# First layer's second MLP product as seven half-size products, and two hand-overs in the MLPs written in another order

## The chip, the cores and the metric

The kernel runs as one program on one core of a Trainium2 chip. The metric is the device time of one execution in microseconds (us). Engines work side by side: TensorE (PE, with the weight loads PEld), VectorE (DVE), ScalarE (ACT), GpSimd (POOL) and SyncE (SP), and 16 DMA engines that all queues share. DMAs are started from SP's, ACT's and POOL's instruction streams. Each engine works through its own instructions in order; a wait at the head of such a stream holds up everything behind it.

## The reference

A two-layer decoder trunk over 1024 tokens with 1024 features. Each layer is a token mixer, an MLP and a gated embedding, each with a norm ahead and a sum behind. Cut to what matters here (per layer `i`):

```python
D_MODEL, SEQ, DEPTH = 1024, 1024, 2
D_FF = 4 * D_MODEL
for i in range(DEPTH):
    hn = rms_norm(h, norm_mix[i])
    y = attention_mixer(hn, ...) if i % 2 == 0 else recurrent_conv_mixer(hn, ...)
    h = h + y
    hn = rms_norm(h, norm_mlp[i])
    h = h + jnp.square(jax.nn.relu(hn @ w_mlp_in[i])) @ w_mlp_out[i]
    hn = rms_norm(h, norm_ple[i])
    h = h + (p[i] @ w_ple_proj[i]) * jax.nn.sigmoid(hn @ w_ple_gate[i])
return rms_norm(h, norm_final)
```

All operands are float32. "The first MLP matrix" is `w_mlp_in` (1024 by 4096), "the second" `w_mlp_out` (4096 by 1024).

## The kernel before

**Tiles.** Everything is held feature-major: 8 blocks of 128 features by 1024 tokens (`h[m]`), and 32 such blocks for the hidden layer. To keep float32 accuracy on TensorE each operand is split into a rounded high part (ScalarE, `hi`, L76) and the rest (VectorE, `lo`, L79, or L89 for weights), and one product of a 128x128 weight block and 512 tokens is three matmuls of 128x512: high by high, high by low, low by high (`mm3`, L92 to L97). A bank is one 128x512 accumulator of PSUM; there are 8 in turn.

**The plain MLP, first layer** (`mlp`, L348). `up` multiplies the input by `w_m1` block by block (48 matmuls a block), scales by the norm (L364), squares what is positive (L365) and splits into `hh`, `hl`. After five blocks eight rounds follow, each with 8 row blocks by two halves of the tokens by four hidden blocks of the second matrix (192 matmuls, and 16 additions into `h`, L385), and four more blocks of `up` between. In all 1536 matmuls belong to the first matrix and 1536 to the second. Woven in is `s5_prep`, a generator that makes tables for the second layer's recurrent mixer in eight parts ("quads"): small VectorE work, then (`later`, one `next` on) 4 transposes (L1111) and 4 small matmuls (L1115) on TensorE, a copy `kt` out of PSUM, eight small DMAs that place `kt` into a zeroed tile `M` (L1127), and a split of `M` that is written to memory (`spill`, L1045 and L1046).

**The MLP of seven products, second layer.** Both matrix products of the second layer are done as 2x2 block products with seven half-size products in place of eight; the sums that this needs are taken on VectorE. Up: `out_proj_halves` and `up_lead` do what needs the first half of the tokens alone, `up_operands` makes the operands X3, X5, X6 from the second half, `up_first` the first sums of weights (`s12`) and products 5 and 6, `up_rest` the operands X4 and X7, `mlp_up` the 16 pairs of hidden blocks; each pair writes its results z1, z2 and four combinations of them to memory (`o1_d`, `o2_d`, `o4_d`). Down: `mlp_down` reads for each of seven products and eight groups a weight tile `raw` and an operand tile `zr` back, splits both, and does 24 matmuls (4 banks by 2 halves by 3); `more(2)` keeps two operand pairs ahead. That makes 56 steps, 1344 matmuls. Its last four blocks of `h` are finished one after another (L765), each with the split for what follows (`xsplit`, L155) and the sum of squares (L304).

**Order.** TensorE's order is that in which the code is written. The order on the other engines is made at build time by a scheduler that goes by readiness and by the code's order; on the chip it is fixed. Pools of SBUF are stacked on a left and a right side; a tile that takes the place of an older one waits until that is free.

**Behind the MLP** come `ple` (first layer: two weight blocks at once, in four banks, inner loop over the eight input blocks) and `ple_last` (second layer: one block at a time).

Of the kernel before, what the change touches and what calls it, by code (L numbers as in the profile page):

```python
# [8 lines left out]
F32 = mybir.dt.float32  # L9
# [9 lines left out]
P = 128  # L19
# [46 lines left out]
class Trunk:  # L66
# [95 lines left out]
    def run(self):  # L162
        tc, nc, A = self.tc, self.nc, self.A
        pool = tc.tile_pool
        with pool(name="w", bufs=1, side=LEFT) as self.wp, \
# [11 lines left out]
            for l in range(2):  # L177
                if l == 0:
                    self.attention(xp)
                with pool(name=f"md{l}", bufs=6, space=PSUM, reuse_waits="tile") as self.mx, ExitStack() as rs:  # L180
# [4 lines left out]
                    if l == 0:  # L185
                        xq = rs.enter_context(pool(name=f"xq{l}", bufs=1, side=RIGHT, reuse_waits="tile"))
                        hp = hs.enter_context(pool(name=f"h{l}", bufs=1, side=RIGHT, reuse_waits="tile"))
                        sp = self.ss.enter_context(pool(name=f"st{l}", bufs=1, side=RIGHT, reuse_waits="tile"))
                        h, xs, st = self.out_proj(l, xp, hp, xq, sp)
                        nxt.close()  # L190
                        with pool(name=f"hid{l}", bufs=1, side=LEFT, reuse_waits="tile") as dp:
                            xs, st = self.mlp(l, h, xs, st, dp, hp, xq)
                        hs.close()
                    else:
                        with pool(name=f"xa{l}", bufs=1, side=RIGHT, reuse_waits="tile") as xa:
# [16 lines left out]
                        xq = rs.enter_context(pool(name=f"xq{l}", bufs=1, side=RIGHT, reuse_waits="tile"))  # L212
                        with pool(name=f"dn{l}", bufs=1, side=LEFT, reuse_waits="tile") as dn:
                            xs, st = self.mlp_down(l, dn, xq)
# [106 lines left out]
    def out_proj(self, l, xp, hp, xq, sp):  # L321
# [14 lines left out]
        def out(m, n, ps):  # L336
# [9 lines left out]
        return h, xs, st  # L346

    def mlp(self, l, h, xs, st, dp, hp, xq):  # L348
        nc, A = self.nc, self.A
        w1 = A["w_m1"][l * FB : (l + 1) * FB]  # L350
        nb = 5 if l == 0 else 6
        hid, nxs, nst, r = {}, [], self.stats_new((xq, "rstd", 1), (dp, "hl", nb)), []

        def up(fb, n, ps):
            if not r:
                if l:
                    self.log_exp()
                r.append(self.rstd_full(st, xq, dp))
                self.ss.close()
            s = slice(n * H, n * H + H)  # L360
            if fb not in hid:
                hid[fb] = [dp.tile([P, T], F32R, tag=x, bufs=nb, name=x) for x in ("hh", "hl")]
            z = dp.tile([P, H], F32, tag="z", bufs=4, name="z")
            nc.vector.tensor_tensor(z, ps, r[0][:, s], ALU.mult)  # L364
            nc.vector.scalar_tensor_tensor(z, z, 0.0, z, ALU.max, ALU.mult)  # L365
            self.hi(hid[fb][0][:, s], z)
            self.lo(hid[fb][1][:, s], z, hid[fb][0][:, s])

        def up_blocks(f0, f1, lead=1):
            self.blocks([w1[f] for f in range(f0, f1)], xs, f1 - f0, list(range(KB)), lambda m, n, ps: up(f0 + m, n, ps), lead)  # L370

        prep = self.s5_prep() if l == 0 else None
        up_blocks(0, 5, 2)
        for c in range(8):
            if prep:
                next(prep)
            for dp2 in range(4):
                w = self.wtile(A["w_m2"][(l * 8 + c) * 4 + dp2])
                for d in range(2):
                    m = 2 * dp2 + d  # L380
                    col = lambda k: tuple(w[j][:, (k - 4 * c) * 256 + d * P : (k - 4 * c) * 256 + d * P + P] for j in range(2))
                    for n in range(2):
                        s = slice(n * H, n * H + H)
                        ps = self.chains([(w, hid, col, n)], list(range(4 * c, 4 * c + 4)))[0]
                        nc.vector.tensor_tensor(h[m][:, s], ps, h[m][:, s], ALU.add)  # L385
                    if c == 7:
                        nc.sync.dma_start(self.h2_d[m], h[m])
                        nxs.append(self.xsplit(h[m], self.gain(3 * l + 2, m), xq))
                        self.stat_block(nst, h[m])
            for f in range(4 * c, 4 * c + 4):  # L390
                del hid[f]
            if c < 7:
                up_blocks(4 * c + 5, min(4 * c + 9, FB))
        if prep:
            for _ in prep:
                pass
        return nxs, nst
# [8 lines left out]
    def split(self, full, pool, tags, bufs):  # L406

        w = full.shape[-1]
        h, l = [pool.tile([P, w], F32R, tag=t, bufs=bufs, name=t) for t in tags]
        self.hi(h, full)  # L410
        self.lo(l, full, h)
        return h, l
# [90 lines left out]
    def put(self, X, p, k, full, xo):  # L503
        X[p, k] = self.split(full, xo, (f"x{p}{k}h", f"x{p}{k}l"), 1)

    def up_operands(self, l, h, st, xo, X):
# [3 lines left out]
        for p in (7, 4):  # L510
            for k in range(4):
                X[p, k] = [xo.tile([P, H], F32R, tag=f"x{p}{k}{x}", bufs=1, name="x") for x in "hl"]
        for k in range(4):
# [3 lines left out]
            self.put(X, 3, k, b[:, rt], xo)  # L517
            v.tensor_tensor(a[:, rt], a[:, rt], a[:, lt], ALU.subtract)
            self.put(X, 5, k, a[:, rt], xo)
            v.tensor_tensor(b[:, rt], b[:, rt], a[:, rt], ALU.subtract)  # L520
            self.put(X, 6, k, b[:, rt], xo)

    def up_rest(self, h, xo, X):
# [3 lines left out]
        for k in range(4):  # L527
            a, b = h[k], h[k + 4]
            for p, s, x, y in ((4, lt, b[:, lt], b[:, rt]), (7, rt, b[:, rt], a[:, lt])):
                v.tensor_tensor(b[:, s], x, y, ALU.subtract)  # L530
                self.hi(X[p, k][0], b[:, s])
                self.lo(X[p, k][1], b[:, s], X[p, k][0])
# [15 lines left out]
    def up_first(self, l, s0, lead, X):  # L548

        raw, a = self.up_raw(l, 0)  # L550
        s12, ops = self.up_s12(a, s0)
# [6 lines left out]
        return raw, a, s12  # L558

    def mlp_up(self, l, X, up, s0, lead, first):  # L560
# [7 lines left out]
        two = lambda d: d.rearrange("p (b e t) -> p b e t", e=2, t=H)  # L568
        both = lambda t: t.rearrange("p (b t) -> p b t", t=H)

        def pair(mp):
            w, bank, c, z = {}, {p: lead[mp, p] for p in (1, 2, 6, 5) if (mp, p) in lead}, {}, {}
            raw, a, s12 = first if mp == 0 else (*self.up_raw(l, mp), None)
            g, e = mp // 2, mp % 2
# [20 lines left out]
            def out(p):  # L595
# [18 lines left out]
                elif p == 3:  # L614
# [4 lines left out]
                    nc.scalar.dma_start(self.o1_d[g][:, e * H : e * H + H], z1[:, lt])  # L619
                else:  # L620
# [4 lines left out]
                    nc.scalar.dma_start(two(self.o2_d[g])[:, :, e, :], both(z2))  # L625
                    ta, tb = [up.tile([P, 1024], F32, tag="tt", bufs=2, name=f"tt{j}") for j in range(2)]
                    tt(ta[:, lt], z1[:, rt], z1[:, lt], ALU.subtract)
                    tt(ta[:, rt], z2[:, rt], ta[:, lt], ALU.subtract)
                    tt(tb[:, lt], z2[:, rt], z1[:, rt], ALU.subtract)
                    tt(tb[:, rt], z2[:, lt], ta[:, rt], ALU.subtract)  # L630
                    for j, t in enumerate((ta, tb)):
                        nc.gpsimd.dma_start(two(self.o4_d[g])[:, 2 * j : 2 * j + 2, e, :], both(t))

            for p in (1, 6, 2, 5, 7, 3, 4):
                if (mp, p) not in lead:
# [3 lines left out]
                    for k in range(4):  # L639
                        self.mm3(bank[b], [o[:, k * P : k * P + P] for o in w[p]], X[p, k], k == 0 and p == b, k == 3, p != b)  # L640
                out(p)

        for mp in range(FB // 2):
            pair(mp)

    def mlp_down(self, l, dn, xq):
# [3 lines left out]
        lt, rt = slice(0, H), slice(H, T)  # L650
        z_d = {1: (self.o1_d, 0), 2: (self.o2_d, 0), 3: (self.o2_d, 1), 5: (self.o4_d, 0), 6: (self.o4_d, 1), 7: (self.o4_d, 2), 4: (self.o4_d, 3)}
# [25 lines left out]
        def operands():  # L677

            for p in (1, 2):
                for g in range(8):  # L680
# [19 lines left out]
        gen, ahead = operands(), []  # L700
# [14 lines left out]
        h, nxs, nst = [], [], self.stats_new((xq, "rstd", 1), (dn, "zr", 3))  # L715
# [7 lines left out]
        for p in (1, 2):  # L723
            for g in range(8):
                step(b1, p == 1 and g == 0, g == 7, p == 2)
                if p == 1 and g in (3, 4):
                    for m in range(g * 4 - 12, g * 4 - 8):
                        h.append(dn.tile([P, T], F32, tag=f"h{m}", bufs=1, name="h"))
# [32 lines left out]
        more(2)  # L761
        for j in range(4):
# [1329 lines left out]
```

## Time and profile before

| | us |
|---|---|
| median of 3 runs (2612.85 to 2615.89) | 2614.22 |
| the profiled execution | 2615.06 |
| its span, first to last instruction | 2613.2 |
| TensorE busy | 2527.2 (97%) |
| VectorE busy | 1693.9 (65%) |
| ScalarE busy | 978.9 (37%) |
| mean granted TensorE clock | 0.988 of full speed |

Stages on the span's clock, from the trace: attention up to about 580 us, the first layer's projection to 661, its MLP 661 to 1393, its gated embedding from there; the recurrent mixer to about 1780, the second layer's MLP up to 2180, down to 2504, the last embedding and the norm to 2613.2.

How to read the rows: a row of the timeline is start, duration, engine, source line, operation, what is written from what, and in brackets how long the engine had been idle and what ended that. Starts of consecutive matmuls give TensorE's pace; their durations overlap. "SPq" rows are DMA issues of SP's stream: the duration is the time that the issue held the stream, not the transfer's. The groups of rows stand below the change.

### The profile page before, as it was taken

How to read it: one execution, taken by the hardware profiler on the slowest of the kernel's cores; microseconds unless marked ns; L12 is line 12 of the kernel's file. 1: busy time of each engine (PE TensorE's matmuls, PEld its weight loads, DVE VectorE, ACT ScalarE, POOL GpSimd, SP SyncE). 2: the span in 40 equal slices, each digit the busy share in tenths (PEclk: the TensorE clock that was granted, in tenths of full speed). 3: DMA queues.
4: the chain of work that ended last, by engine and by line, in shares of the span. 5: the costliest groups of instructions: out<-in, count | busy, mean ns of one | idle time of the engine just before them, and what ended most of it. 6: DMA issues, size and time to landing. Idle time of an engine off the chain costs nothing.

```text
span 2613.2 us, 32842 instructions
## 1 busy us (share of the span) xinstructions
PE 2527.2 (97%) x12296; PEld 2090.7 (80%) x12296; DVE 1693.9 (65%) x3225; ACT 978.9 (37%) x1531; POOL 102.6 (4%) x88
## 2 busy tenths in 40 slices
PE   8999999989999999999999999999799998999998
PEld 6788888878888888888888897887588887888877
DVE  6776756544856556645667778666676664568776
ACT  5554556443311211211134433334454444333444
POOL 1111110000000000000000000000000000000000
PEclk9999999989999999999999999999899999999999
DMA  5443423361122112212225655353353447778652
GB/s 175 112 125 105 142 74 105 83 215 58 37 81 85 61 65 85 70 58 83 85 96 173 222 167 169 129 200 131 121 193 133 157 154 268 258 235 276 209 181 96
DMA packets 156207, 357.53 MB, mean 137 GB/s; under 512 B 21904, under 2 KB 53904, under 8 KB 156048
## 3 DMA queue, kind: packets, MB, share of 16 engines
q1 hardware_dynamic: 139776, 313.22, 36.7%
q0 software_dynamic: 7040, 25.17, 2.5%
q10 hardware_dynamic: 9232, 17.04, 1.7%
q8 instruction: 97, 1.59, 0.3%
q14 instruction: 62, 0.51, 0.1%
HBM read 238.83 MB, written 90.18 MB: 126 GB/s over the span
## 4 chain that ended last, share of the span: by engine, by line
PE 88%; DVE 6%; ACT 2%; issue 1%; DMA 0%; SPq 0%; DVEq 0%; ACTq 0%
PE mm L95 27%; PE mm L97 27%; PE mm L96 27%; PE tp L1911 2%; PE S L1878 1%; PE S L1879 1%; PE o L1936 1%; PE o L1935 1%; DVE zl L79 1%; PE S L2003 1%; DVE p L1881 1%; DVE p L1900 0%; DVE tl L79 0%; DMA ql<-zl 0%; PE mm L1115 0%
## 5 line engine op out<-in xcount | busy, mean ns | idle before, releaser
L95 PE MATMUL mm<-xh,wh 128*128 128x512 f32 (+1 forms) x1504 | 587.3, 390 | 0.0
L97 PE MATMUL mm<-xh,wl 128*128 128x512 f32 (+1 forms) x1504 | 582.1, 387 | 2.7 <-DVE wl L89 2.7
L96 PE MATMUL mm<-xl,wh 128*128 128x512 f32 (+1 forms) x1504 | 580.2, 386 | 1.6 <-DVE xl L155 1.6
L76 ACT ACTIVATE wh<-wr 128x1024 fp32r<-128x1024 f32 (+1 forms) x167 | 175.8, 1054 | 557.0 <-PE mm L96 480.8
L97 PEld LDWEIGHTS mm<-xh,wl 128*128 128x128 f32 x1504 | 283.6, 189 | 66.1 <-DVE wl L89 3.2
L96 PEld LDWEIGHTS mm<-xl,wh 128*128 128x128 f32 x1504 | 283.7, 189 | 61.4 <-DVE xl L155 2.0
L95 PEld LDWEIGHTS mm<-xh,wh 128*128 128x128 f32 x1504 | 283.6, 189 | 58.0 <-ACT sph L76 0.2
L95 PE MATMUL mm<-hh,wh 128*128 128x512 f32 x512 | 203.7, 398 | 0.0
L97 PE MATMUL mm<-hh,wl 128*128 128x512 f32 x512 | 203.0, 397 | 0.0
L96 PE MATMUL mm<-hl,wh 128*128 128x512 f32 x512 | 203.0, 396 | 0.0
L89 DVE TENSOR_TENSOR wl<-wr,wh 128x1024 fp32r<-128x1024 f32 x130 | 158.6, 1221 | 52.2 <-ACT wh L76 51.4
L95 PE MATMUL mm<-zh,wh 128*128 128x512 f32 x448 | 178.5, 398 | 5.9 <-ACT zh L76 5.9
L96 PE MATMUL mm<-zl,wh 128*128 128x512 f32 x448 | 178.5, 398 | 0.8 <-DVE zl L79 0.8
L97 PE MATMUL mm<-zh,wl 128*128 128x512 f32 x448 | 178.3, 398 | 0.0
L385 DVE TENSOR_TENSOR h<-mm,h 128x512 f32<-128x512 f32 x128 | 88.3, 690 | 95.3 <-PE mm L97 94.0
L364 DVE TENSOR_TENSOR z<-mm,rstd 128x512 f32<-128x512 f32 x64 | 44.1, 692 | 150.0 <-PE mm L97 150.0
L1886 ACT ACTIVATE p<-p,m 128x128 f32<-128x128 f32 (+7 forms) x128 | 99.0, 774 | 97.3 <-DVE m L1881 96.2
L95 PEld LDWEIGHTS mm<-hh,wh 128*128 128x128 f32 x512 | 96.4, 188 | 24.6 <-issue 1.5
L97 PEld LDWEIGHTS mm<-hh,wl 128*128 128x128 f32 x512 | 96.5, 188 | 23.5
L96 PEld LDWEIGHTS mm<-hl,wh 128*128 128x128 f32 x512 | 96.5, 188 | 23.2
L95 PE MATMUL mm<-wh,xh 128*128 128x256 f32 x384 | 112.5, 293 | 2.1 <-DVE v L1635 1.4
L97 PE MATMUL mm<-wh,xl 128*128 128x256 f32 x384 | 109.7, 286 | 0.0
(629 smaller groups left out, 4860.5 us busy)
## 6 DMA issues: line engine op xcount, KB each, us to landing
wr<-w_m SPq DMA_DIRECT2D x99, 512.0 KB, 3.4
raw<-w_m SPq DMA_DIRECT2D x80, 512.0 KB, 5.6
s<-s SPq DMA_DIRECT2D x64, 256.0 KB, 4.4
ot<-tt POOLq DMA_DIRECT2D x32, 512.0 KB, 5.2
zr<-ot SPq DMA_DIRECT2D x32, 512.0 KB, 4.5
wr<-w_out SPq DMA_DIRECT2D x24, 512.0 KB, 3.5
q<-zh SPq DMA_DIRECT2D x64, 128.0 KB, 2.3
ql<-zl SPq DMA_DIRECT2D x64, 128.0 KB, 2.3
```

What stands on the lines that cost most here:

```text
L76: self.nc.scalar.activation(out, in_, AF.Copy, scale=scale)
L79: self.nc.vector.tensor_tensor(out, full, hi.bitcast(F32), ALU.subtract)
L89: self.weng.tensor_tensor(l, raw, h.bitcast(F32), ALU.subtract)
L95: mm(ps, L[0], R[0], start=first, stop=False)
L96: mm(ps, L[0], R[1], start=False, stop=False)
L97: mm(ps, L[1], R[0], start=False, stop=last)
L364: nc.vector.tensor_tensor(z, ps, r[0][:, s], ALU.mult)
L385: nc.vector.tensor_tensor(h[m][:, s], ps, h[m][:, s], ALU.add)
L1878: nc.tensor.matmul(S, qh, qk["k"][c][:, k], start=True, stop=False)
L1879: nc.tensor.matmul(S, ql, qk["k"][c][:, k], start=False, stop=True)
L1886: nc.scalar.activation(pt[:, :w], pt[:, :w], AF.Exp, bias=m, scale=-1.0, accum_out=den)
L1911: nc.tensor.transpose(tps[:, off + n * P : off + n * P + P], maps[j][:, kb * P : kb * P + P], self.ident)
```

## The change

- `mlp` goes. The first layer's up product is `mlp_up_plain`: the same 1536 matmuls, but it writes its hidden blocks to memory as the second layer does (`z_out`, now shared), and calls the generator after blocks 1, 3, 7, ..., 31, nine times. `out_proj` writes `h[m]` to memory (`h1_d`), since `h` no longer stays.
- The first layer's down product is `mlp_down`, which both layers now use; `w_m2` of the first layer is laid out as that of the second.
- `down_lead` loads and splits the first operand pair of `mlp_down` (in tiles `wr` and `sf`, `sh`, `sl` that exist already); `mlp_down` takes it as `first`. In the first layer it is called after the last up block, in the second after product 7 of the last pair.
- Second layer: `up_raw` and `up_s12` of the first pair stand ahead of `up_operands`; all X tiles are allocated at once in the order 7, 4, 6, 5, 3; `mlp_down` allocates its eight `h` tiles first.
- The first weight tile of the gated embedding is asked for (`pre`) ahead of the last two steps of `mlp_down`.

```diff
@@ run
...
-                        h, xs, st = self.out_proj(l, xp, hp, xq, sp)
...
-                            xs, st = self.mlp(l, h, xs, st, dp, hp, xq)
+                            xs, st = self.out_proj(l, xp, hp, xu, sp)
...
+                                first = self.mlp_up_plain(l, xs, st, cu, xu, hs)
@@
-                                self.up_operands(l, h, st, xo, X)
+                                for p in (7, 4, 6, 5, 3):
+                                    for k in range(4):
+                                        X[p, k] = [xo.tile([P, H], F32R, tag=f"x{p}{k}{x}", bufs=1, name=f"x{p}{k}{x}") for x in "hl"]
                                 with pool(name=f"s0{l}", bufs=1, side=LEFT, reuse_waits="tile") as s0:
-                                    first = self.up_first(l, s0, lead, X)
-                                    self.up_rest(h, xo, X)
+                                    raw, a = self.up_raw(l, 0)
+                                    s12, ops = self.up_s12(a, s0)
+                                    self.up_operands(l, h, st, X)
+                                    self.up_first(lead, ops, X)
+                                    self.up_rest(h, X)
...
-                                        self.mlp_up(l, X, up, s0, lead, first)
+                                        first = self.mlp_up(l, X, up, s0, lead, (raw, a, s12))
-                            xs, st = self.mlp_down(l, dn, xq)
+                        xs, st, pre = self.mlp_down(l, dn, xq, first)
@@ out_proj
             if n:
+                nc.sync.dma_start(self.h1_d[m], h[m])
@@
+    def mlp_up_plain(self, l, xs, st, cu, xu, hs):
...
+        def out(m, n, ps):
...
+            nc.vector.tensor_tensor(z[m][:, s], ps, r[0][:, s], ALU.mult)
+            if n:
+                nc.scalar.activation(z[m], z[m], AF.Relu)
+                nc.scalar.activation(z[m], z[m], AF.Square)
+            if m % 2 and n:
+                if m == FB - 1:
+                    first.append(self.down_lead(l, self.s0))
+                self.z_out(m // 2, z.pop(m - 1), z.pop(m), cu)
+                if m == 1 or m % 4 == 3:
+                    next(prep, None)
+
+        with self.tc.tile_pool(name=f"s0{l}", bufs=1, side=LEFT, reuse_waits="tile") as self.s0:
...
+            prep = self.s5_prep()
+            self.blocks(A["w_m1"][l * FB : (l + 1) * FB], xs, FB, list(range(KB)), out)
+            for _ in prep:
                 pass
-        return nxs, nst
+        return first[0]
@@ mlp_up (its code for the results of a pair is now z_out)
+                if mp == FB // 2 - 1 and p == 7:
+                    nxt.append(self.down_lead(l, s0))
                 out(p)
...
+    def z_out(self, mp, z1, z2, pool):
...
+        nc.scalar.dma_start(self.o1_d[g][:, e * H : e * H + H], z1[:, lt])
+        nc.scalar.dma_start(two(self.o2_d[g]), both(z2))
+        ta, tb = [pool.tile([P, 1024], F32, tag="tt", bufs=2, name=f"tt{j}") for j in range(2)]
+        tt(ta[:, lt], z1[:, rt], z1[:, lt], ALU.subtract)
+        tt(ta[:, rt], z2[:, rt], ta[:, lt], ALU.subtract)
+        tt(tb[:, lt], z2[:, rt], z1[:, rt], ALU.subtract)
+        tt(tb[:, rt], z2[:, lt], ta[:, rt], ALU.subtract)
+        for j, t in enumerate((ta, tb)):
+            nc.gpsimd.dma_start(two(self.o4_d[g])[:, 2 * j : 2 * j + 2], both(t))
+
+    def down_lead(self, l, s0):
+
+        nc = self.nc
+        raw = self.wp.tile([P, 1024], F32, tag="wr", bufs=2, name="wr")
+        nc.sync.dma_start(raw, self.A["w_m2"][l * 32])
+        z = s0.tile([P, 1024], F32, tag="sf", bufs=1, name="zr")
+        nc.sync.dma_start(z, self.o1_d[0])
+        return self.split(raw, self.wp, ("wh", "wl"), 3), self.split(z, s0, ("sh", "sl"), 1)
@@ mlp_down
+    def mlp_down(self, l, dn, xq, first):
+        h = [dn.tile([P, T], F32, tag=f"h{m}", bufs=1, name="h") for m in range(KB)]
...
-                for g in range(8):
+                for g in range(p == 1, 8):
                     yield wop(a(1, p, g)), zop(p, g)
...
-        gen, ahead = operands(), []
+        gen, ahead = operands(), [first]
...
         more(2)
+        pre = [self.wtile(A["w_pg"][l * KB])]
         for j in range(4):
...
-        return nxs, nst
+        return nxs, nst, pre
@@ ple
-        self.blocks(A["w_pg"][l * KB : (l + 1) * KB], xs, KB, list(range(KB)), out)
+        self.blocks(A["w_pg"][l * KB : (l + 1) * KB], xs, KB, list(range(KB)), out, pre=pre)
```

SP's stream behind the last quad of the tables (first layer, end of the MLP before, end of the up product now; `s_7_...` are the quad's tables in memory, `ho` and `pp` inputs of the gated embedding). Before:

```order
L83 DMA wr<-w_pg 128x1024
L1127 DMA M<-kt 16x512
...
L1127 DMA M<-kt 16x4x16
L83 DMA wr<-w_pg 128x1024
L1045 DMA s_7_0_159<-sph 128x512
L1046 DMA s_7_1_160<-spl 128x512
L780 DMA ho<-hm_207 128x1024
```

Now:

```order
L1129 DMA M<-kt 16x512
...
L1129 DMA M<-kt 16x4x16
L1047 DMA s_7_0_159<-sph 128x512
L1048 DMA s_7_1_160<-spl 128x512
L657 DMA raw<-w_m 128x1024
L663 DMA zr<-oa_184 128x1024
L657 DMA raw<-w_m 128x1024
L663 DMA zr<-oa_185 128x1024
```

Behind the quad's two writes there now stand the loads of the second operand pair of the down product (`raw`, `zr` of group 1; the pair of group 0 is `down_lead`'s and is loaded earlier).

VectorE at the end of the first layer's MLP (`h` the sums, `xl` the splits for the gated embedding, `acc` the sum of squares, `wl` its weights). Before:

```order
L385 TENSOR_TENSOR h<-mm,h 128x512
L155 SCALAR_TENSOR_TENSOR xl<-h,gains,xh 128x1024
L304 TENSOR_TENSOR acc<-acc,sq 128x1024
L385 TENSOR_TENSOR h<-mm,h 128x512
L89 TENSOR_TENSOR wl<-wr,wh 128x1024
L79 TENSOR_TENSOR spl<-mm,sph 128x512
L155 SCALAR_TENSOR_TENSOR xl<-h,gains,xh 128x1024
```

Now:

```order
L89 TENSOR_TENSOR wl<-wr,wh 128x1024
L767 TENSOR_TENSOR h<-mm,h 128x512
L155 SCALAR_TENSOR_TENSOR xl<-h,gains,xh 128x1024
L308 TENSOR_TENSOR acc<-acc,sq 128x1024
L767 TENSOR_TENSOR h<-mm,h 128x512 x2
L155 SCALAR_TENSOR_TENSOR xl<-h,gains,xh 128x1024
L308 TENSOR_TENSOR acc<-acc,sq 128x1024
L155 SCALAR_TENSOR_TENSOR xl<-h,gains,xh 128x1024
L308 TENSOR_TENSOR acc<-acc,sq 128x1024
L767 TENSOR_TENSOR h<-mm,h 128x512
L89 TENSOR_TENSOR wl<-wr,wh 128x1024 x2
L155 SCALAR_TENSOR_TENSOR xl<-h,gains,xh 128x1024
```

The first `wl` is that of the gated embedding's first weight block; that of its second stands behind all four sums.

VectorE at the start of the second layer's up product (`s` sums of weights, `x..l` operands). Before:

```order
L530 TENSOR_TENSOR h<-h 128x512
L79 TENSOR_TENSOR x<-h,x 128x512 x2
L590 TENSOR_TENSOR s_16853<-wr 128x512
L591 TENSOR_TENSOR s_16853<-wr,s_16791 128x512
L79 TENSOR_TENSOR al<-wr,ah 128x512
L601 TENSOR_TENSOR u_16866<-mm,u_16864 128x512
```

Now:

```order
L515 TENSOR_TENSOR h<-h 128x512
L79 TENSOR_TENSOR x43l<-h,x43h 128x512
L79 TENSOR_TENSOR x73l<-h,x73h 128x512
L568 TENSOR_TENSOR s_17028<-wr 128x512
L569 TENSOR_TENSOR s_17028<-wr,s_16926 128x512
L79 TENSOR_TENSOR al<-wr,ah 128x512
L579 TENSOR_TENSOR u_17041<-mm,u_17039 128x512
```

The operands X4 and X7 of `up_rest` stand ahead of the second sums of weights (`s34`) in both.

## Rows read from the trace of the kernel before

**Rows 1.** The page: the chain's shares by engine.

```profile
PE 88%; DVE 6%; ACT 2%; issue 1%; DMA 0%; SPq 0%; DVEq 0%; ACTq 0%
```

**Rows 2.** Windows: stretch, its us, then PE, PEld, DVE, ACT, POOL busy, clock, DMA share, GB/s.

```profile
660.00:1391.40 731.40, 731.40 (x3165) 587.02 (x3164) 444.75 (x1082) 151.09 (x204) 0.00 (x0) 1.00 0.23 75
2186.40:2191.60 5.20, 4.33 (x10) 3.10 (x11) 4.77 (x5) 3.20 (x4) 0.36 (x1) 0.51 1.02 380
```

**Rows 3.** Waits of TensorE, 1780 to the end: us in total, times, longest.

```profile
PE mm L95 <- ACT sh L76: 10.2, 1, 10.2
```

**Rows 4.** TensorE's timeline: second layer's hand-over, and its down product's last matmul.

```profile
2180.19 0.39 PE L97 MATMUL mm<-x,al 128*128 128x512 f32 x1
2186.47 0.80 PE L95 MATMUL mm<-zh,wh 128*128 128x512 f32 x1 [5.90 <-ACT zh L76]
2188.07 0.79 PE L96 MATMUL mm<-zl,wh 128*128 128x512 f32 x1 [0.80 <-DVE zl L79]
...
2191.59 0.39 PE L95 MATMUL mm<-zh,wh 128*128 128x512 f32 x1
...
2504.12 0.40 PE L97 MATMUL mm<-zh,wl 128*128 128x512 f32 x1
```

**Rows 5.** Groups by line, the page: matmuls of the two down products.

```profile
L95 PE MATMUL mm<-hh,wh 128*128 128x512 f32 x512 | 203.7, 398 | 0.0
L95 PE MATMUL mm<-zh,wh 128*128 128x512 f32 x448 | 178.5, 398 | 5.9 <-ACT zh L76 5.9
```

**Rows 6.** Groups by line: VectorE, 660 to 1391.4.

```profile
L385 DVE TENSOR_TENSOR h<-mm,h 128x512 f32<-128x512 f32 x127 | 87.6, 690 | 95.3 <-PE mm L97 94.0
L89 DVE TENSOR_TENSOR wl<-wr,wh 128x1024 fp32r<-128x1024 f32 x63 | 76.8, 1221 | 5.0 <-ACT wh L76 4.2
L365 DVE SCALAR_TENSOR_TENSOR z<-z 128x512 f32<-128x512 f32 x64 | 44.2, 693 | 1.8
```

**Rows 7.** TensorE's timeline, the last quad of the tables.

```profile
1391.42 0.60 PE L1111 MATMUL mm<-ident,Gt 128*128 128x128 f32 x4
1392.93 0.50 PE L95 MATMUL mm<-xh,wh 128*128 128x512 f32 x1
```

**Rows 8.** The same quad on ScalarE, VectorE and SP's stream.

```profile
1394.82 0.55 ACT L1119 COPY kt<-mm 16x512 f32<-16x512 f32 x1
1403.21 0.63 ACT L76 ACTIVATE sph<-M 128x512 fp32r<-128x512 f32 x1 [7.83 <-DMA M<-kt]
1396.41 0.20 DVE L1124 TENSOR_TENSOR kt<-kt,di 16x64 f32<-16x64 f32 x1
1396.64 5.06 SPq L1127 DMA_DIRECT2D M<-kt  x8
1404.97 0.45 SPq L780 DMA_DIRECT2D ho<-hm  x1
```

**Rows 9.** Second layer's hand-over on SP's stream, ScalarE and VectorE.

```profile
2180.61 0.33 SPq L661 DMA_DIRECT2D zr<-oa  x1
2182.76 1.06 ACT L624 ACTIVATE z<-z 128x1024 f32<-128x1024 f32 x1
2185.38 1.04 ACT L76 ACTIVATE zh<-zr 128x1024 fp32r<-128x1024 f32 x1
2186.79 1.22 DVE L79 TENSOR_TENSOR zl<-zr,zh 128x1024 fp32r<-128x1024 f32 x1
```

**Rows 10.** DMA issues by line (KB each, median us from issue to landing).

```profile
zr<-oa SPq DMA_DIRECT2D x8, 512.0 KB, 6.6
```

**Rows 11.** End of the second layer's down product on ScalarE and VectorE.

```profile
2505.08 2.00 ACT L76 ACTIVATE wh<-wr 128x1024 fp32r<-128x1024 f32 x2
2507.61 2.35 DVE L89 TENSOR_TENSOR wl<-wr,wh 128x1024 fp32r<-128x1024 f32 x2
```

**Rows 12.** Start of the second layer's up product: VectorE, TensorE.

```profile
1887.39 0.69 DVE L590 TENSOR_TENSOR s<-wr 128x512 f32<-128x512 f32 x1
1889.88 0.80 PE L95 MATMUL mm<-x,sh 128*128 128x512 f32 x1 [10.23 <-ACT sh L76]
```

More of the change, by code (lines that the diff above doesn't have):

```diff
@@ L355, in up @@
             if not r:
-                if l:
-                    self.log_exp()
-                r.append(self.rstd_full(st, xq, dp))
+                r.append(self.rstd_full(st, xu, cu))
                 self.ss.close()
+                hs.close()
             s = slice(n * H, n * H + H)
[L361 to L393, printed above, removed]
@@ L394, in mlp @@
-        if prep:
+            if m not in z:
+                z[m] = cu.tile([P, T], F32, tag="zp", bufs=4, name="z")
+            nc.vector.tensor_tensor(z[m][:, s], ps, r[0][:, s], ALU.mult)
[8 more added lines that the diff above has]
+                    next(prep, None)
@@ L408, in split, with split_to @@
         w = full.shape[-1]
[L409 to L412, printed above, removed]
+        ops = [pool.tile([P, w], F32R, tag=t, bufs=bufs, name=t) for t in tags]
+        self.split_to(ops, full)
+        return ops
+    def split_to(self, ops, full):
+        self.hi(ops[0], full)
+        self.lo(ops[1], full, ops[0])
     def out_proj_halves(self, l, xp, hp, sp, xa, X):
@@ L501, in up_lead, with up_operands @@
         return lead
-    def put(self, X, p, k, full, xo):
-        X[p, k] = self.split(full, xo, (f"x{p}{k}h", f"x{p}{k}l"), 1)
-    def up_operands(self, l, h, st, xo, X):
+    def up_operands(self, l, h, st, X):
         v = self.nc.vector
         lt, rt = slice(0, H), slice(H, T)
-        for p in (7, 4):
-            for k in range(4):
-                X[p, k] = [xo.tile([P, H], F32R, tag=f"x{p}{k}{x}", bufs=1, name="x") for x in "hl"]
         for k in range(4):
@@ L546, in up_s12, with up_first @@
         return s12, self.split(s12, s0, ("sh", "sl"), 1)
-    def up_first(self, l, s0, lead, X):
-        raw, a = self.up_raw(l, 0)
-        s12, ops = self.up_s12(a, s0)
+    def up_first(self, lead, ops, X):
         for p in (6, 5):
@@ L567, in mlp_up @@
         self.bn = 7
-        two = lambda d: d.rearrange("p (b e t) -> p b e t", e=2, t=H)
-        both = lambda t: t.rearrange("p (b t) -> p b t", t=H)
         def pair(mp):
@@ L624, in out @@
                     nc.scalar.activation(z2, z2, AF.Square)
[L625 to L632, printed above, removed]
+                    self.z_out(mp, z1, z2, up)
             for p in (1, 6, 2, 5, 7, 3, 4):
@@ L640, in pair @@
                         self.mm3(bank[b], [o[:, k * P : k * P + P] for o in w[p]], X[p, k], k == 0 and p == b, k == 3, p != b)
+                if mp == FB // 2 - 1 and p == 7:
+                    nxt.append(self.down_lead(l, s0))
                 out(p)
+        nxt = []
         for mp in range(FB // 2):
             pair(mp)
-    def mlp_down(self, l, dn, xq):
+        return nxt[0]
+    def z_out(self, mp, z1, z2, pool):
+        nc = self.nc
+        tt = nc.vector.tensor_tensor
+        lt, rt = slice(0, H), slice(H, T)
+        g, e = mp // 2, mp % 2
+        two = lambda d: d.rearrange("p (b e t) -> p b e t", e=2, t=H)[:, :, e, :]
+        both = lambda t: t.rearrange("p (b t) -> p b t", t=H)
+        nc.scalar.dma_start(self.o1_d[g][:, e * H : e * H + H], z1[:, lt])
[8 more added lines that the diff above has]
+    def down_lead(self, l, s0):
+        nc = self.nc
+        raw = self.wp.tile([P, 1024], F32, tag="wr", bufs=2, name="wr")
[4 more added lines that the diff above has]
+    def mlp_down(self, l, dn, xq, first):
         nc, A = self.nc, self.A
```

56 lines of the change are left out of this document (24 added, 32 removed).

## The prediction

> **What bounds the kernel now.** I read the chain of waits first, then the windows, then the list of what TensorE waits for, and last the timelines where the change moves something. The chain lies on TensorE for 88% of the span [rows 1]. Over the first layer's MLP TensorE is busy in all of its 731.4 us at a granted clock of 1.00, while VectorE has 444.75 us of work, 61%, and the DMA engines 23% [rows 2]. So the number of matmuls sets the time there, and taking matmuls away shortens the span for as long as the other engines and the transfers keep up. From 1780 us to the end TensorE has two long waits: 10.2 us for the sums of weights early in the second layer's up product [rows 3, 12], and 5.90 us at the hand-over between that layer's up and down products, where the first operand pair has first to be read back and split [rows 4]. The timelines there and at the last quad of the tables [rows 4, 7 to 9] give the prices below.
>
> **The change part by part.** All terms are against the profiled execution, 2615.06 us; it is 0.84 above the median of 2614.22, which I take off at the end.
>
> *Fewer matmuls, −45.0.* The first layer's down product falls from 3 x 512 to 3 x 448 matmuls of 128x512 [rows 5], 192 fewer. Their pace I take from the second layer's down product, which is the same code: from the 10th matmul at 2191.59 to the 1344th at 2504.12 are 1334 intervals in 312.53 us [rows 4], 0.2343 us each. That is 192 x 0.2343 = 45.0. As this is unbroken from start to end, the loads and splits of the down product keep up once it runs; the first layer's has the same steps.
> The Trainium skill ("TensorE: Matmul & The Clock Gate", Part 1, "Wait — 56ns, not 53.3ns?") gives 215.7 ns for a warm 128x512 matmul in a row. By it this term would be 41.4; the trace has 0.2343, and the measurement decides.
>
> *The up product of the first layer, 0.* Its 1536 matmuls stay. What is new beside them must be hidden in 1536 x 0.2343 = 360 us instead of 731. Before, VectorE had 444.75 us there. Of this go 128 sums into `h` (0.690 each), 32 `wl` of the second matrix (1.221) and 128 operations of 0.69 for the square and the split; 64 sums of 128x512 for what is written to memory come in [rows 2, 6]: 444.75 − 88.3 − 39.1 − 88.5 + 44.2 = 273.1 us, 76% of 360, or 34.1 of each 45.0 us that hold four blocks and a quad. ScalarE gets a relu and a square of 1.06 each [rows 9] for every block, 32 x 2.12 = 68 us on top of 151, and loses splits. Both stay below TensorE, so I take nothing; the end above is priced in the rivals.
>
> *The first layer's hand-over, +13.8.* Before, the last quad's work stood beside other matmuls and cost TensorE only its own. Now it is asked for after the last up block, and SP's stream, ScalarE and VectorE all have it ahead of the second operand pair of the down product. Count from the start of its transposes (t = 0, 1391.42 before).
> - TensorE goes on with matmuls at t = 1.5 (1392.93, [rows 7]) and has the first product, loaded ahead: 24 x 0.2343 = 5.6 us, so until t = 7.1.
> - On ScalarE stand behind the small matmuls a relu (1.06) and the copy `kt` (0.55): t = 3.1. VectorE adds 0.20: t = 3.3 [rows 8, 9].
> - Eight DMAs put `kt` into `M`. They hold SP for 5.06 us, and ScalarE could split `M` at 1403.21, 6.6 after the addition had ended at 1396.61: t = 9.9.
> - The split is written out, and SP's next issue behind that came at 1404.97, 1.8 later [rows 8]. This is now `raw` of the second pair: t = 11.7, and `zr` one issue (0.45) later, t = 12.1.
> - From the issue of such a `zr` to the start of its split were 4.8 us (2180.61 to 2185.38, [rows 9]); the median to landing is 6.6 [rows 10]. I take 4.8, since that pair too stood at a hand-over and not in the middle of the product: t = 16.9, and 1.0 for `zh`: 17.9.
> So TensorE stands from 7.1 to 17.9, 10.8 us. Behind such a stop it is slow: the first nine intervals of the second layer's down product took 5.12 us (2186.47 to 2191.59) against 2.11 at full pace, with the granted clock at 0.51, the lower of the two levels, and a wait for `zl` among them [rows 2, 4]. That is 3.0 more, 13.8 in all. Ends: nothing, if the pair's transfers start ahead of the quad's; 15.6 with the landing of 6.6.
> The Trainium skill ("DMA: Bandwidth & Descriptors", "Anatomy of one DMA — SWDGE (gpsimd) path") has about 2.0 us fixed and 50 ns a dispatch. `M` would then be there 8 x 0.05 + 2.0 = 2.4 us after the addition, the stop 4.2 shorter and the predicted time about 2574. The trace shows 6.6, and these DMAs are issued by SP and not by GpSimd; the measurement decides.
>
> *The first layer's gated embedding, +2.6.* The first weight block is now asked for ahead of the last two steps, but this stage begins with two blocks at once, and the order puts the second block's `wl` behind the four last sums of `h`. The same place in the second layer is the model [rows 4, 11]: with the next stage at 2504.35, its first six matmuls end at 2505.76. The second `wh` would be there 1.0 after 2505.08, at 2506.1: 0.35 lost. Its `wl`, first of the two begun at 2507.61 (2.35 for both, 1.2 each), ends at 2508.8, wanted by the third matmul at 2506.6: 2.2. Ends: 0 if VectorE gets to it sooner, 5.5 with a low clock (about 3 as above) behind the stop.
>
> *The second layer's hand-over, −7.2.* Before, TensorE's last up matmul gave way at 2180.42 (2180.19 + 0.23), the next started at 2186.47: 6.05 lost, and 3.0 by the slow start, 9.05 in all. Now the first pair is there, and its 5.6 us run from 2180.42 to 2186.04. The second pair has the place that the first had: `zr` waits for the last results to be written (their square starts at 2182.76), its `zh` is split from 2185.38 and `zl` ends at 2188.0 [rows 9]. TensorE loses 0.43 to the first `zh` (2186.47 − 2186.04) and 1.37 to `zl` (wanted at 2186.70): 1.8. So −7.2, between −9.05 (no loss left) and −5 (a low clock for half of what follows, about 2).
>
> *The second layer's up product, 0.* The sums for the first products go ahead of the operands, but the order of VectorE ahead of the second sums (`s34`) is as before: the operands X4 and X7 first. TensorE's 10.2 us are a wait for these second sums (begun at 1887.39, TensorE goes on at 1889.88, [rows 12]). Ends: −12 when that wait goes with some of the slow start behind it; +2 when the earlier first sums delay the operands by three operations of 0.69. I take 0, since the instructions ahead of the wait are the same.
>
> Writing `h` out in the projection is eight transfers of 512 KB that no instruction of that stage waits for; the second layer's end keeps its order. Both 0. Sum: −45.0 + 13.8 + 2.6 − 7.2 = −35.8. From 2615.06 that gives 2579.3, and in the frame of the median 2614.22 − 35.8 = 2578.4.
>
> **The rivals.** *The hand-over is covered:* the quad's work behind the last block is over sooner than before, since fewer instructions stand beside it. The order on SP, with the pair behind the quad's writes, speaks against it. Then 5 us or less is lost and the time is 2565 to 2570.
> *The second layer's up product gains too:* the operands have their tiles without waiting, all steps come earlier, and the 10.2 us and some 3 of slow clock go: 2578.4 − 13.2 = 2565. The unchanged order of VectorE speaks against it.
> *More is lost in the first layer, and it is still faster:* in its up product TensorE waits a little at quads, or the second pair lands late behind the writes of the last hidden blocks. Up to 30 us, 2587 to 2609. The doubled density of work beside TensorE speaks for it, the shares of 76% and less against.
> *Slower:* VectorE becomes the bound in the first layer's up product. Transposes of a quad stand in TensorE's stream at a fixed place and wait for tables that VectorE makes among the blocks' own operations. It decides from 35.8 / 8 = 4.5 us lost at each of the eight quads, that is from 49.5 us of work for VectorE in each period of 45.0, where I count 34.1. At 55 us a period, 10 lost at each of eight, it would be 2578.4 + 80 = 2658.
>
> **How the numbers follow.** Forecast 0.62 (2572 to 2587), hand-over covered 0.14, second layer's start gains 0.07, more lost but faster 0.12, slower 0.05. No change, within 0.2% or 5.2 us, which is about what a measurement of this kernel can tell, needs 30 to 41 us lost that I don't see: 0.02, out of the third rival and the border of the last. So faster 0.93, same 0.02, slower 0.05. Range: 2564 to 2594; it takes in the term of 13.8 from nothing to its double, and leaves out two thirds of the third rival, the last one and the far ends.
>
> **What would show it.** In the first layer's down product 1344 matmuls at 0.234 us; one stop of about 11 us behind its 24th matmul, released by `zh`, with `raw` and `zr` on SP behind the writes of the last quad; a small wait for `wl` at the start of the gated embedding; at the second layer's hand-over no stop over 2 us; the 10.2 us still there. It is wrong if TensorE waits at the quads' transposes, or if the stop behind the first product is missing.

## The result and the profile after

The changed kernel takes 2593.48 us (median of 4 runs, 2592.61 to 2594.79) against 2615.05 for the kernel before (4 runs, 2612.85 to 2617.35): a ratio of 0.9918, interval 0.9901 to 0.9935, 21.6 us less. The forecast was 35.8 less. The profiled execution has a span of 2590.9, 22.3 shorter than before.

TensorE's waits over the whole span of the changed kernel (us in total, times, longest), as [rows 3]; of the list, those that belong to this case:

```profile
PE mm L95 <- ACT zh L76: 12.9, 2, 12.6
PE mm L95 <- ACT sh L76: 10.2, 1, 10.2
...
PE mm L97 <- DVE st L1094: 8.7, 1, 8.7
...
PE mm L97 <- DVE wl L89: 4.7, 2, 2.7
```

Of these the 10.2 stood there before, and one 2.7 for `wl`. The 5.90 of the second layer's hand-over is gone [rows 4]. New are 12.6 for `zh`, at the first layer's hand-over, and 8.7 under the name of `st`, which no step of the prediction has. TensorE's timeline of the changed kernel at these two places:

```profile
696.23 0.39 PE L96 MATMUL mm<-xl,wh 128*128 128x512 f32 x1
705.29 0.80 PE L97 MATMUL mm<-xh,wl 128*128 128x512 f32 x1 [8.68 <-DVE st L1094]
...
710.86 0.39 PE L95 MATMUL mm<-xh,wh 128*128 128x512 f32 x1
...
1043.39 0.60 PE L1113 MATMUL mm<-ident,Gt 128*128 128x128 f32 x4
...
1050.39 0.39 PE L97 MATMUL mm<-sh,wl 128*128 128x512 f32 x1
1063.40 0.80 PE L95 MATMUL mm<-zh,wh 128*128 128x512 f32 x1 [12.61 <-ACT zh L76]
...
1069.08 0.40 PE L97 MATMUL mm<-zh,wl 128*128 128x512 f32 x1
```

*The stop that was not forecast.* The matmul at 705.29 multiplies by `wl`, the low part of the up product's fourth weight block; `st`, named in brackets, only ended at the same time and is no operand of it. VectorE and ScalarE of the changed kernel ahead of it (`wh` is the high part of this block):

```profile
682.43 1.06 ACT L76 ACTIVATE wh<-wr 128x1024 fp32r<-128x1024 f32 x1 [1.62 <-PE mm L96]
684.52 0.69 DVE L137 TENSOR_SCALAR rs_v<-mm 128x512 f32<-128x512 f32 x1 [1.35 <-PE mm L119]
...
694.38 0.68 DVE L1080 TENSOR_TENSOR Gt<-rv,bb 128x512 f32<-128x512 f32 x1
701.16 0.75 DVE L1081 TENSOR_TENSOR CA<-CA,om 128x576 f32<-128x576 f32 x1
704.02 1.22 DVE L89 TENSOR_TENSOR wl<-wr,wh 128x1024 fp32r<-128x1024 f32 x1
```

`wh` was done at 683.5. VectorE stood idle then, until 684.52, for the norm's sums, which come next in its order; `wl` began only at 704.02, behind the first quad's tables (`Gt`, `CA`). In the kernel before the same split stood ahead of them:

```profile
683.00 1.23 DVE L89 TENSOR_TENSOR wl<-wr,wh 128x1024 fp32r<-128x1024 f32 x1 [1.23 <-ACT wh L76]
```

The cause is the place of the call in the code: before, `s5_prep` was asked for its first quad after five up blocks, now after two. In the 20 us from 684 to 704 VectorE has no room to make up for it. The windows (columns as in [rows 2]) of the changed kernel, and of the kernel before:

```profile
684.00:704.00 20.00, 12.62 (x55) 9.81 (x53) 19.48 (x65) 9.46 (x18) 1.67 (x2) 0.91 0.27 99
...
720.00:1043.00 323.00, 323.00 (x1417) 258.76 (x1416) 206.24 (x592) 102.28 (x117) 20.34 (x28) 1.00 0.51 176
```

```profile
684.00:704.00 20.00, 20.00 (x87) 16.08 (x86) 20.00 (x41) 9.06 (x19) 0.00 (x0) 1.00 0.17 53
```

VectorE is busy for 19.48 and for 20.00 of these 20 us: in the changed kernel with the norm's chain, the first results and the set-up of the tables, before with the splits of the hidden blocks in place of much of that set-up. Only behind that is its share lower, 206.24 of 323 us, 64%, with TensorE busy without a gap. The stop costs 705.29 − 696.46 = 8.8, and the 13 intervals from 705.29 to 710.86 take 5.57 in place of 3.05: 2.5. Sum 11.4.

*The hand-over.* SP's stream and ScalarE of the changed kernel, as [rows 8] and [rows 9]:

```profile
1046.31 7.20 SPq L1129 DMA_DIRECT2D M<-kt  x8
...
1056.75 0.32 SPq L1048 DMA_DIRECT2D s<-spl  x1
1057.47 0.33 SPq L657 DMA_DIRECT2D raw<-w_m  x1
1057.99 0.32 SPq L663 DMA_DIRECT2D zr<-oa  x1
```

```profile
1055.37 0.63 ACT L76 ACTIVATE sph<-M 128x512 fp32r<-128x512 f32 x1 [8.38 <-DMA M<-kt]
...
1062.29 1.06 ACT L76 ACTIVATE zh<-zr 128x1024 fp32r<-128x1024 f32 x1 [0.18 <-DMA zr<-oa]
```

From the transposes (1043.39) the steps are: `M` split at t = 12.0 (forecast 9.9; the eight DMAs held SP for 7.2 in place of 5.06), `raw` issued at 14.1 (11.7), `zh` done at 20.0 (17.9). TensorE lost 1063.40 − 1050.62 = 12.8, and 3.1 by 11 slow intervals (5.68 against 2.58, a wait of 0.46 for `zl` among them): 15.9.

*The other places* of the changed kernel on TensorE: the last matmul of the first layer's down product, the gated embedding behind it, the second layer's up product (as in [rows 12]) and its hand-over (as in [rows 4]):

```profile
1375.53 0.39 PE L97 MATMUL mm<-zh,wl 128*128 128x512 f32 x1
...
1377.58 0.50 PE L95 MATMUL mm<-xh,wh 128*128 128x512 f32 x1 [0.26 <-ACT wh L76]
1380.29 0.50 PE L97 MATMUL mm<-xh,wl 128*128 128x512 f32 x1 [1.98 <-DVE wl L89]
...
1875.66 0.80 PE L95 MATMUL mm<-x70h,sh 128*128 128x512 f32 x1 [10.23 <-ACT sh L76]
...
2171.71 0.40 PE L97 MATMUL mm<-sh,wl 128*128 128x512 f32 x1
2172.39 0.50 PE L95 MATMUL mm<-zh,wh 128*128 128x512 f32 x1 [0.29 <-ACT zh L76]
2173.98 0.50 PE L96 MATMUL mm<-zl,wh 128*128 128x512 f32 x1 [1.09 <-DVE zl L79]
```

From 1069.08 to 1375.53 the down product's remaining 1308 intervals took 306.45 us, 0.2343 each, as forecast. At the gated embedding TensorE lost 0.43 for `wh` (it could have started at 1377.15) and 2.14 for `wl` (wanted at 1378.15): 2.6.

### The profile page after: what moved, and what is told of

It is laid out like the page before. It is cut to its first block, busy times and chain, and to the rows that moved or that the text cites. A ratio compares the mean times of both kernels' runs of the same rounds, so it can differ in the third digit from the quotient of the medians.

```text
span 2590.9 us, 33012 instructions
## 1 busy us (share of the span) xinstructions
PE 2489.8 (96%) x12104; PEld 2058.3 (79%) x12104; DVE 1724.5 (67%) x3189; ACT 1083.5 (42%) x1615; POOL 131.1 (5%) x128
## 4 chain that ended last, share of the span: by engine, by line
PE 87%; DVE 8%; ACT 2%; issue 1%; DMA 1%; SPq 0%; DVEq 0%; ACTq 0%
PE mm L95 26%; PE mm L97 26%; PE mm L96 26%; PE tp L1913 2%; PE S L1880 1%; PE S L1881 1%; PE o L1938 1%; PE o L1937 1%; DVE zl L79 1%; DVE p L1883 1%; PE S L2005 1%; DVE tl L79 0%; DVE p L1902 0%; DVE wl L89 0%; DMA ql<-zl 0%
## 5 line engine op out<-in xcount | busy, mean ns | idle before, releaser
L95 PE MATMUL mm<-zh,wh 128*128 128x512 f32 x880 | 350.1, 398 | 12.9 <-ACT zh L76 12.9
L96 PE MATMUL mm<-zl,wh 128*128 128x512 f32 x880 | 350.0, 398 | 1.6 <-DVE zl L79 1.6
L97 PE MATMUL mm<-zh,wl 128*128 128x512 f32 x880 | 349.5, 397 | 0.0
L95 PEld LDWEIGHTS mm<-zh,wh 128*128 128x128 f32 x880 | 166.3, 189 | 54.3 <-ACT zh L76 13.8
L96 PEld LDWEIGHTS mm<-zl,wh 128*128 128x128 f32 x880 | 166.3, 189 | 42.9 <-DVE zl L79 2.4
L97 PEld LDWEIGHTS mm<-zh,wl 128*128 128x128 f32 x880 | 166.3, 189 | 40.5
L79 DVE TENSOR_TENSOR wl<-raw,wh 128x1024 fp32r<-128x1024 f32 x78 | 95.3, 1222 | 98.6 <-ACT wh L76 98.4
L79 DVE TENSOR_TENSOR zl<-zr,zh 128x1024 fp32r<-128x1024 f32 x110 | 134.0, 1218 | 2.4 <-ACT zh L76 2.2
L76 ACT ACTIVATE zh<-zr 128x1024 fp32r<-128x1024 f32 x110 | 115.0, 1045 | 0.8 <-DMA zr<-oa 0.8
L96 PE MATMUL mm<-wl,xh 128*128 128x256 f32 x384 | 108.8, 283 | 0.0
```

The source lines that it names most:

```text
L76: self.nc.scalar.activation(out, in_, AF.Copy, scale=scale)
L79: self.nc.vector.tensor_tensor(out, full, hi.bitcast(F32), ALU.subtract)
L95: mm(ps, L[0], R[0], start=first, stop=False)
L96: mm(ps, L[0], R[1], start=False, stop=False)
L97: mm(ps, L[1], R[0], start=False, stop=last)
```

## Experiments

Ahead of the change the profiles differ by up to 5.6 us (its first sums start between 680.21, in experiment 4, and 685.79, in experiment 8), so for single stages I compare "the stretch": from the first matmul of the sums of squares at the first layer's up product to that at its gated embedding. In the kernel before these start at 683.35 and 1415.44; the two rows of the changed one:

```profile
683.86 0.39 PE L118 MATMUL mm<-rs_a,ones 128*128 128x512 f32 x1
...
1400.92 0.39 PE L118 MATMUL mm<-rs_a,ones 128*128 128x512 f32 x1
```

| kernel | median us | ratio to before (interval) | stretch us |
|---|---|---|---|
| before | 2615.05 | | 732.1 |
| changed | 2593.48 | 0.9918 (0.9901 to 0.9935) | 717.1 |
| 1, last quad early | 2586.21 | 0.9893 (0.9879 to 0.9907) | 713.6 |
| 2, first quad late | 2578.44 | 0.9864 (0.9847 to 0.9880) | 705.1 |
| 3, both | 2579.44 | 0.9866 (0.9852 to 0.9879) | 704.3 |
| 4, last quad on another queue | 2591.86 | 0.9913 (0.9900 to 0.9927) | 717.3 |
| 5, no lead in the second layer | 2597.83 | 0.9938 (0.9922 to 0.9955) | |
| 6, first sums late | 2590.50 | 0.9907 (0.9892 to 0.9922) | |
| 7, as 1, own place | 2576.87 | 0.9856 (0.9842 to 0.9871) | 702.2 |
| 8, as 3, own place | 2569.02 | 0.9825 (0.9810 to 0.9839) | 692.9 |

Each ratio is to the kernel before as it was timed together with that kernel: a median of 2615.05 for the changed one, 2614.59 for experiments 1 to 4, 2615.63 for 5 to 8.

**1. The last quad early.**

```diff
-                if m == 1 or m % 4 == 3:
-                    next(prep, None)
+            if n and m in (1, 3, 7, 11, 15, 18, 21, 25, 29):
+                next(prep, None)
```

> Edit: the generator of the tables is called after up blocks 1, 3, 7, 11, 15, 18, 21, 25, 29 in place of 1, 3, 7, ..., 31, so the last quad's transposes, its eight DMAs into M and its two writes stand two blocks (22.5 us) ahead of the end of the first layer's up product. Theory (the stop behind the first down product comes from the last quad, which has SP, ScalarE and VectorE ahead of the second operand pair): the wait of 12.6 us for zh falls to 4 us or less and the slow start behind it goes with it, median about 2593.5 - 13 = 2580 (2577 to 2585). The first quad's stop of 8.7 us for wl stays as it is. Rival (the second pair waits for its tiles, which only the last up block sets free, or for its own transfers): the wait stays above 9 us and the time within 4 us of 2593.5.

The stop fell from 12.6 to 9.3 only, as the rival said. The time, 2586.21, suits neither: it is 7.3 less than the changed kernel's, but the stretch is only 3.5 shorter, and in the profiled execution 1.9 of the rest are of the stages ahead. TensorE, and SP's stream, of this kernel:

```profile
1048.26 0.40 PE L96 MATMUL mm<-sl,wh 128*128 128x512 f32 x1
1048.50 0.39 PE L97 MATMUL mm<-sh,wl 128*128 128x512 f32 x1
1058.16 0.79 PE L95 MATMUL mm<-zh,wh 128*128 128x512 f32 x1 [9.27 <-ACT zh L76]
```

```profile
1033.42 0.32 SPq L1048 DMA_DIRECT2D s<-spl  x1
1048.69 0.33 SPq L657 DMA_DIRECT2D raw<-w_m  x1
```

The quad's last write was issued at 1033.42 and `raw` stood next on SP, yet it went out 15 us later, 0.03 behind the last matmul that reads `sl`, the low part of the preloaded operand (1048.26 + 0.40). So a second wait lay behind the one that I had named. In the layout of the built program the first tile `raw` lies exactly where `sl` lies. The sums `tt` of the last pair, done at 1048.1, or the last writes to memory could be the cause as well; experiment 7 tells them apart.

**2. The first quad late, 3. both.** The same edit with (5, 9, 12, 15, 18, 21, 24, 27, 31), and with (5, 8, 11, 14, 17, 20, 23, 26, 29).

> Edit: the generator of the tables is called after up blocks 5, 9, 12, 15, 18, 21, 24, 27, 31: the first call four blocks later, the last where it was, in between mostly three blocks apart in place of four. Theory (the stop of 8.7 us at the start of the first layer's up product is one of order: VectorE has the first quad's tables ahead of the low part wl of the fourth weight block, whose high part was ready 20 us before): the 8.7 us go and some 2.5 us of slow matmuls behind them, median about 2593.5 - 11 = 2582 (2579 to 2586); the stop at the hand-over stays near 12.6 us. Rival (VectorE has more work there than fits beside TensorE, the order only decides where it shows): with quads closer together TensorE waits 8 us or more elsewhere in that product, and the time stays within 4 us of 2593.5 or rises.

> Edit: the generator is called after up blocks 5, 8, 11, ..., 29, so the first call is later and the last quad earlier. Theory: both stops go, the gains add up to about 24 us, median 2569 to 2572 (2565 to 2575). Rival (VectorE's load is the limit with a quad every three blocks, 33.8 us): TensorE waits in the middle of the up product and less than 15 us are gained.

In 2 the stop of 8.7 is gone and the stretch is 12.0 shorter, against 11 expected; the median fell by 15.0, to 0.6 below the range expected, and in the profiled execution 2.8 of its gain are of the stages ahead. VectorE of experiment 2, and TensorE's waits in its first layer's MLP:

```profile
680.71 1.22 DVE L89 TENSOR_TENSOR wl<-wr,wh 128x1024 fp32r<-128x1024 f32 x1 [1.22 <-ACT wh L76]
...
702.41 0.69 DVE L1081 TENSOR_TENSOR Gt<-Gt,om 128x512 f32<-128x512 f32 x1
```

```profile
PE mm L95 <- ACT zh L76: 12.4, 1, 12.4
```

`wl` stands ahead of `Gt` again and starts at 680.71. With quads three blocks apart TensorE has no gap in 310 us of experiment 3 and VectorE is busy for 72% of them:

```profile
690.00:1000.00 310.00, 310.00 (x1366) 248.09 (x1366) 223.47 (x687) 104.75 (x127) 20.58 (x28) 1.00 0.53 185
```

So the stop was one of order and not of VectorE's load. In 3 the hand-over keeps 9.1, as in 1, for the reason found there, and of the expected 24 only 14.0 came. Over 2 its stretch gains 0.8 and its median nothing: the stop is 3.3 shorter, but slow matmuls behind it and behind the gated embedding's wait took back 2.5 (more on these in the last section).

**4. The last quad by another queue.**

```diff
-                nc.sync.dma_start(m4[...], k4[...])
+                (nc.gpsimd if q == 7 else nc.sync).dma_start(m4[...], k4[...])
```

The writes of its split go the same way.

> Edit: for the last quad alone, the eight DMAs into M and the two writes of its split are issued by GpSimd in place of SP; nothing moves otherwise. If only SP's order kept the second pair back, its loads start some 10 us sooner and the stop of 12.6 us falls to about 7, since ScalarE's order still has the split of M (12.0 us after the transposes) ahead of the two splits of 1.06 each: median about 2593.5 - 5.5 = 2588. If ScalarE's order and the time that M takes are the whole of it, or the DMAs by GpSimd take longer, the stop stays at 12 us or grows and the time is 2592 to 2598.

The stop grew to 13.1, as the second branch has it, with a time 0.1 below that branch's range. SP's stream, VectorE and TensorE of this kernel:

```profile
1046.94 0.33 SPq L657 DMA_DIRECT2D raw<-w_m  x1
1055.08 0.32 SPq L663 DMA_DIRECT2D zr<-oa  x1
```

```profile
1054.36 0.69 DVE L79 TENSOR_TENSOR spl<-M,sph 128x512 fp32r<-128x512 f32 x1 [9.08 <-ACT sph L76]
```

```profile
1046.51 0.40 PE L96 MATMUL mm<-sl,wh 128*128 128x512 f32 x1
1046.75 0.39 PE L97 MATMUL mm<-sh,wl 128*128 128x512 f32 x1
1060.21 0.80 PE L95 MATMUL mm<-zh,wh 128*128 128x512 f32 x1 [13.08 <-ACT zh L76]
```

With nothing ahead of it on SP, `raw` went out 0.03 behind the last matmul that reads `sl` (1046.51 + 0.40), and `zr` waited on until 1055.08, 0.03 behind VectorE's split of `M` (1054.36 + 0.69), over whose place it lies. `M` itself came later by GpSimd: ScalarE split it at t = 13.9, in place of 12.0. Both branches of my expectation had only orders and the time of the DMAs in view; the places of the tiles decide as well.

**7 and 8. Another place for `raw`.** The calls of 1 and of 3, and in `mlp_down`:

```diff
         h = [dn.tile([P, T], F32, tag=f"h{m}", bufs=1, name="h") for m in range(KB)]
+        dn.tile([P, 1024], F32, tag="sf", bufs=2, name="sf")
```

That lays the two tiles `sf` out ahead of `raw`, which then lies behind `sl`. The other tiles for weights and operands of `mlp_down` move with it.

> Edit: the last quad early as in the first experiment, and in mlp_down the two tiles for sums of weights are laid out ahead of the tiles raw, so that the first raw no longer lies where the first operand pair's low part sl lies. Theory (with the quad out of the way the second pair's load waits for that place, which the first down product frees with its last matmuls: raw was issued at 1048.69, the last matmul on sl stood just ahead of 1048.50): raw and zr are issued 10 us or more ahead of the end of the first product, the stop falls from 9.3 to under 2 us, and the slow start goes too: 12 us less than the 2586.2 of the first experiment, median about 2574 (2571 to 2578). Rival (the late issue comes from the sums tt of the last pair on VectorE or from the writes to memory, done at about the same time): the stop stays above 7 us and the time near 2586.

> Edit: both quads moved as in the third experiment (calls after blocks 5, 8, ..., 29), and the tiles laid out as in the seventh. Theory: no stop over 2 us left in the first layer's MLP; 12 us less than 2579.4, median about 2567 (2563 to 2572). Rival: as for the seventh, no more than 3 us less than 2579.4.

SP's stream and TensorE of experiment 7:

```profile
1033.65 0.43 SPq L658 DMA_DIRECT2D raw<-w_m  x1
```

```profile
1048.77 0.49 PE L95 MATMUL mm<-zh,wh 128*128 128x512 f32 x1
1050.31 0.50 PE L96 MATMUL mm<-zl,wh 128*128 128x512 f32 x1 [1.05 <-DVE zl L79]
```

`raw` goes out at 1033.65, though the sums `tt` of the last pair end at 1048 and its writes are issued from 1046 on here too, so the rival falls. Of the stop 0.2 for `zh` and 1.05 for `zl` are left, and the stretch is 11.4 shorter than in 1. Experiment 8 has neither stop: 2569.02 us, 24.5 less than the changed kernel and 0.9825 of the kernel before. It is the fastest of all. Its waits in the first layer's MLP:

```profile
PE mm L97 <- DVE wl L89: 2.0, 1, 2.0
PE mm L96 <- DVE zl L79: 1.0, 1, 1.0
PE mm L95 <- ACT wh L76: 0.2, 1, 0.2
```

**5. No lead in the second layer.**

```diff
-                    nxt.append(self.down_lead(l, s0))
+                    nxt.append(None)
-        gen, ahead = operands(), [first]
+        gen, ahead = operands(), [first] if first else []
```

> Edit: in the second layer down_lead is left out, mlp_down loads its first operand pair itself, as before; the first layer keeps it. Theory (the preloaded pair is worth the difference of the hand-overs, 9.05 us lost before and 1.8 now): TensorE again waits about 6 us for zh behind the last up matmul and some 3 us are lost in a slow start, +7.2 against the changed kernel, median about 2600.7 (2597 to 2604). Rival (the second pair is as late as the first was, so the lead only moves the wait): within 3 us of 2593.5.

TensorE waits 5.92 again, as in [rows 4]:

```profile
2169.46 0.80 PE L95 MATMUL mm<-zh,wh 128*128 128x512 f32 x1 [5.92 <-ACT zh L76]
```

Between the same matmuls ahead of and behind the hand-over (the norm's sums at 1831.94 and 2522.98 before) the kernel before took 691.04, this one 691.05 and the changed one 684.01: the lead is worth 7.0. The medians show 4.4 of it. In the profiled execution the stages ahead are 0.8 shorter here, and the first layer's stretch is 1.8 shorter (715.3): behind its two stops matmuls were slow for 3.0 and 4.3 us, in place of 5.6 and 5.7.

**6. The first sums late.**

```diff
+                                    self.up_operands(l, h, st, X)
                                     raw, a = self.up_raw(l, 0)
                                     s12, ops = self.up_s12(a, s0)
-                                    self.up_operands(l, h, st, X)
```

> Edit: in the second layer the loads and the first sums of weights of pair 0 (up_raw, up_s12) stand behind up_operands again; the tiles of X stay as they are. Theory: no change, 2593.5 (2590 to 2597), since TensorE waits for the operands X5 and X6 and later, 10.2 us, for the second sums; both waits keep their lengths within 1 us. Rival (the early first sums are what lets products 5 and 6 start): the waits for the first sums grow by 2 us or more and the time by as much.

2590.50, no slower. The waits for X5 and for the second sums are 2.23 and 10.23 us in both, and between the norm's sums named under 5 lie 683.92 us, against 684.01 in the changed kernel. That part of the change does nothing that can be measured.

## Why the prediction was right in its direction and short in its size

The time fell, but by 21.6 in place of 35.8. The range of 2564 to 2594 held it by 0.5 us only, which is luck: the time lies outside the 2572 to 2587 of the forecast's own case, in the 2587 to 2609 of the rival "more is lost in the first layer". Of the signs, the stop behind the first product, the wait for `wl`, the short second hand-over and the 10.2 came as told. Term by term:

| term | forecast | measured | from |
|---|---|---|---|
| fewer matmuls | −45.0 | −45.0 | 192 at the 0.2343 measured, no gap beside the stops |
| first layer's up product | 0 | +11.4 | stop behind 696.23 |
| first layer's hand-over | +13.8 | +15.9 | stop behind 1050.39 |
| gated embedding | +2.6 | +2.6 | 0.43 + 2.14 |
| second layer's hand-over | −7.2 | −7.0 | experiment 5 |
| second layer's up product | 0 | 0 | 10.23, experiment 6 |

The first four give −45.0 + 11.4 + 15.9 + 2.6 = −15.1, and the stretch is 15.0 shorter. With −7.0 that is −22.1; the span fell by 22.3.

- *The step that failed* is "The up product of the first layer, 0". I let VectorE's mean share of 76% stand for every place in the stage. At its start VectorE is all but full for 20 us, and there the order decides: the move of the first call from behind five blocks to behind two put a split that TensorE waits for behind tables that nobody waits for yet. The rival "more is lost in the first layer" named waits at quads as one of its ways, but with a chance of 0.12, and looked for them at the transposes; it was a weight block that came late. Experiment 2 took the stop away by the places of the calls alone. The rival in which VectorE is the bound of the whole product is refuted by experiment 3.
- *The hand-over* was right in mechanism and 2.1 short: the eight DMAs into `M` held SP for 7.2 us and not 5.06. All eight quads show this: their DMAs held SP for 7.1 to 9.9 in the changed kernel and for 5.05 to 5.40 before. The 16 DMA engines were busy for 78% of these 7.2 us, and for 44% of the 5.06 before; that this load is the cause is not shown. What I had not seen is that a second wait stood right behind, for the place of `sl`. It cost nothing in the changed kernel, since it ended first (with the last matmul that reads `sl`, at 1050.6, against 1057.47), but it kept most of the stop when the quad was moved.
- *The second layer's hand-over* came out as worked: 0.45 (2172.39 − 2171.94) for `zh` and 1.36 (2173.98 − 2172.62) for `zl`, 1.8 left as forecast.

## What to carry to other kernels

A mean share of an engine over a stage says nothing of its start: look at the stretch where a new call lands, and read in the order what stands ahead of the operand that the bound engine needs next. Work without a due time (tables for a later stage) belongs behind such an operand, and away from a hand-over. When a queue's order is mended and the stop stays, look at what lies in the same place of memory: the tile that a load fills may still be read by the very product that the load was meant to hide behind.

## What the runs showed of the hardware

Behind the two new stops of the changed kernel TensorE ran at the lower of its two clock levels for 5.6 and 5.7 us: granted clock 0.51 and 0.50 in these windows, where matmuls start 0.43 apart.

```profile
705.20:710.80 5.60, 5.51 (x13) 4.35 (x14) 5.06 (x34) 1.54 (x2) 0.00 (x0) 0.51 0.59 174
1063.30:1069.00 5.70, 5.14 (x11) 3.76 (x12) 4.31 (x5) 3.65 (x5) 0.00 (x0) 0.50 1.02 403
```

That is 2.5 and 3.1 us on top of the waits (0.46 of the second is a wait for `zl`). The length is not fixed: behind the same two stops matmuls were slow for 3.0 and 4.3 us in experiment 5, and for 6.9 behind the hand-over of experiment 3. Behind the 2.0 us at the gated embedding the clock stayed up in the changed kernel (1.00 from 1380.2 to 1384.0), but in experiments 3 and 8 matmuls stood 0.43 apart there for 3.5 and 3.3 us (1.7 and 1.4 lost; granted clock 0.52 in experiment 8 from 1357.8 to 1361.2). What makes the difference stays open.
